# Moving the adaLN sums of one transformer block to other places among the gate logits and the levels of a triangular solve

## The chip, the cores and the metric

The kernel runs on one core of one Trainium2 chip, as one launch. The metric is device time in microseconds (us). A profile of one execution goes with it: which instruction ran on which engine and when, and what each wait ended with. The engines are TensorE (PE in the rows; PEld is its weight load), VectorE (DVE), ScalarE (ACT), GpSimd (POOL) and SyncE (SP), which issues the transfers from HBM. Each engine takes its own instructions in a fixed order, so a waiting instruction holds up all that stand behind it.

## The reference

256 tokens of width 1024 pass two layers. What matters here is the first layer's modulation (adaLN) and its gated delta rule.

```python
mod = jax.nn.silu(c) @ w_ada[l] + b_ada[l]            # c: 1 x 1024, w_ada: 1024 x 6144
shift1, scale1, gate1, shift2, scale2, gate2 = jnp.split(mod, 6, axis=-1)
h = modulate(rmsnorm(x, norm1_w[l]), shift1, scale1)
proj = h @ w_in[l]                                    # ..., d_q, d_k, d_v, d_z, d_a, d_b
qkv = silu(causal_dwconv(concat([d_q, d_k, d_v]), conv_w[l]))
beta = jax.nn.sigmoid(d_b)
g = -jnp.exp(a_log[l]) * jax.nn.softplus(d_a + dt_bias[l])
...
# gated_delta_rule, in chunks
decay = jnp.exp(jnp.where(tri_incl, g[..., :, None] - g[..., None, :], -jnp.inf))
a_mat = jnp.where(tri_strict, (k_beta @ swapaxes(k)) * decay, 0.0)
t_mat = lax.linalg.triangular_solve(eye + a_mat, eye, lower=True, unit_diagonal=True)
u = t_mat @ v_beta
...
x = x + gate1 * mix
ffn = hierarchical_moe(modulate(rmsnorm(x, norm2_w[l]), shift2, scale2), ...)
x = x + gate2 * ffn
```

After it come retention, the output projection, the router, 32 experts, a pooling mixer and a convolutional feed-forward layer.

## The kernel before

**The adaLN sums.** The 6144 columns of `w_ada` are twelve pieces of 512 columns (2 MB each), numbered 0 to 11. Pieces 0 to 3 (shift1, scale1) are needed for the first projection and are summed before it. Pieces 4 and 5 (gate1), 6 and 7 (shift2), 8 and 9 (scale2) and 10 and 11 (gate2) are needed much later: gate1 after the output projection, the others at the router or in the experts. A piece j has two steps. `s j` (`ada_sum`) is eight matmuls on TensorE (line 382), with the weight piece as the moving operand, and one VectorE instruction that takes the result out of PSUM: for the row pieces 4, 5, 10, 11 an addition onto `acc` (line 385), for the others a transpose (line 387). `e j` (`ada_end`) finishes it: for a row piece one matmul against ones (line 417) and a copy to `g1b` or `g2b`, by VectorE or ScalarE in turn (line 208 or 210); for a column piece four small matmuls (line 408) and an addition into `modT` (line 411).

**Where they stand.** The table `ADA` names places in the program and the steps put there; `ada("L1")` performs those of the place L1. The Tile scheduler then fixes each engine's order, so a step may slide past neighbours, and other work fills in around it.

```python
ADA = {'L1': 's4 s5', 'L2': 'e4', 'L3': 's6', 'L4': 'e5', 'L5': 's7 e6', 'E': 'e7', 'F': 's10', ...}
```

**The stage around it.** After the first projection (k, lines 509 and 568) come the gate logits: `psab` (line 605), its copy `abT` (line 208), two matmuls (line 611 before, 612 after), and a chain of small VectorE instructions with two exponentials on ScalarE (lines 613 to 638) that ends in `gg`. From `gg` come the decays `Dm` (lines 651 to 661) and the matrix `Am` (line 689). The solve inverts 32x32 blocks in five levels, 0 to 4: each is 32 tiny matmuls `Zc,Am` (line 705 before, 706 after), a masked product `Q` on VectorE (line 716), 32 tiny matmuls `Q,Xc` (none at level 0), a subtraction into `Zc` (line 723) and a transpose (line 725), after which stands the place `L0` to `L4`. Joining the blocks follows (lines 735 to 771, place `L5` in the middle), then the products with v (lines 783 to 808; the place `E` is ahead of line 788).

**What fills in.** The projections of v and then of q run beside it as `products`: triples of matmuls of 256 columns (line 290). Each piece of weights (128x512) is first split into a high part `wh` on ScalarE (line 281) and a low part `wl` on GpSimd (line 284). There are four buffers of each (NFS=4), so the sixth split waits until the products of the second are done. The convolution of v (line 568, three taps for each of four parts, on VectorE; lines 562, 563, 571 on ScalarE) runs there as well.

**Loads.** Weights lie in rings of 2 MB slots. SyncE issues the loads in one fixed order (`LOADS`), each when its slot is free: piece 8 goes into the slot of piece 4, w1 of `w_in` into that of piece 6, and so on, and the expert weights stand behind them.

Of the kernel before, what the change touches and what calls it, by code (L numbers as in the profile page):

```python
# [32 lines left out]
L4 = 5  # L33
# [12 lines left out]
SLOTS_MOE = 'ehg'  # L46
ADA_ACT = ()
SIDE = {3: 8, 7: 9}
ADA = {'L1': 's4 s5', 'L2': 'e4', 'L3': 's6', 'L4': 'e5', 'L5': 's7 e6', 'E': 'e7', 'F': 's10', 'G': 'e10', 'J': 's11', 'K': 'e11'}
KPOOL = ()  # L50
VPRE = 2
NLATE = 3
# [127 lines left out]
def build(ctx, tc, io, out, dbg=None):  # L180
    nc = tc.nc
    V, S, G, PE = nc.vector, nc.scalar, nc.gpsimd, nc.tensor
# [8 lines left out]
    def bank(tag=None):  # L191
        return pp.tile([128, 512], F32, name="ps", tag=tag or ptag[0])
# [12 lines left out]
    def copy(dst, src):  # L205
        _alt[0] ^= 1
        if _alt[0]:
            V.tensor_copy(dst, src)
        else:
            S.activation(dst, src, AF.Copy)  # L210
# [182 lines left out]
    def ada_sum(j, rows=False):  # L393
        for _ in ada_steps(j, rows, False):
            pass
# [58 lines left out]
    def ada(at):  # L454

        for step in ADA.get(at, "").split():
            j = int(step[1:])
            if step[0] == "s":
                ada_sum(j, j in (4, 5, 10, 11))
            else:  # L460
                ada_end(j)

    def ada_end(j):
        if j in (4, 5, 10, 11):
            ada_rows(j, (g1b if j < 6 else g2b)[:, 512 * (j % 2 if j > 9 else j - 4):][:, :512])
        else:
            ada_cols(j)
# [138 lines left out]
                      start=kk == 0, stop=kk == 1)  # L606
    abT = dp.tile([128, T], F32, name="abT")
    copy(abT, psab[:, :T])
    psab2 = bank()
    for t in range(2):  # L610
        PE.matmul(psab2[:, 8 * t:8 * t + 8], lhsT=abT[:, 128 * t:128 * t + 128], rhs=cfv("sel32"), start=True, stop=True)
# [727 lines left out]
    def tt(shape, name, bufs=None, tag=None, dtype=F32):  # L1339
        return tl.tile(shape, dtype, name=name, tag=tag or name, **({"bufs": bufs} if bufs else {}))  # L1340
# [7 lines left out]
    s4 = tt([128, 2, 2], "s4")  # L1348
    s5 = tt([128, 2, 2], "s5")
# [184 lines left out]
```

## Time and profile before

| what | us |
|---|---|
| median of three runs | 896.58 |
| lowest and highest | 892.93, 896.63 |
| the profiled execution | 897.43 |
| its span, first to last instruction | 895.6 |
| experts begin (first matmul of line 1285) | about 253 |
| gate logits and solve (lines 611 to 788) | about 53 to 106 |

TensorE is busy for 848.5 us of the span (95%), VectorE 398.5, ScalarE 272.5, GpSimd 146.6. In a row of the timeline the first number is the start in us, the second how long it (or the merged run of xN) took; brackets tell the idle time of the engine before it and what ended it. fp32 matmuls appear as two records each, so eight matmuls of line 382 are x16.

### The profile page before, as it was taken

How to read it: one execution, taken by the hardware profiler on the slowest of the kernel's cores; microseconds unless marked ns; L12 is line 12 of the kernel's file. 1: busy time of each engine (PE TensorE's matmuls, PEld its weight loads, DVE VectorE, ACT ScalarE, POOL GpSimd, SP SyncE). 2: the span in 40 equal slices, each digit the busy share in tenths (PEclk: the TensorE clock that was granted, in tenths of full speed). 3: DMA queues.
4: the chain of work that ended last, by engine and by line, in shares of the span. 5: the costliest groups of instructions: out<-in, count | busy, mean ns of one | idle time of the engine just before them, and what ended most of it. 6: DMA issues, size and time to landing. Idle time of an engine off the chain costs nothing.

```text
span 895.6 us, 12945 instructions
## 1 busy us (share of the span) xinstructions
PE 848.5 (95%) x5337; PEld 537.7 (60%) x5337; DVE 398.5 (44%) x750; ACT 272.5 (30%) x512; POOL 146.6 (16%) x109
## 2 busy tenths in 40 slices
PE   3998999989989999999999998989998999999998
PEld 0685788767734334343443444334334999999996
DVE  2577587586512122221222221122214877666664
ACT  2243154364401101010110101001015565555552
POOL 0234331162000000000000000000000033523525
PEclk9988899999999999999999999999999999999999
DMA  9982769767589999999999999999999744453001
GB/s 374 420 359 97 283 255 380 289 256 324 189 314 412 420 429 430 427 426 429 426 428 430 425 430 425 429 426 429 415 410 428 331 187 190 165 211 142 1 2 47
DMA packets 26111, 288.54 MB, mean 322 GB/s; under 512 B 3008, under 2 KB 3264, under 8 KB 9792
## 3 DMA queue, kind: packets, MB, share of 16 engines
q1 hardware_dynamic: 26048, 287.66, 78.1%
q8 instruction: 44, 0.72, 0.3%
q14 instruction: 19, 0.16, 0.1%
HBM read 286.60 MB, written 1.05 MB: 321 GB/s over the span
## 4 chain that ended last, share of the span: by engine, by line
PE 56%; DMA 14%; DVE 1%; ACT 0%; issue 0%; SPq 0%
PE ps L290 21%; PE ps L1285 18%; DMA wt<-in_w 14%; PE ps L1313 9%; PE ps L1244 3%; PE ps L1221 2%; PE ps L1396 1%; PE ps L1301 1%; PE ps L1415 1%; PE ps L1051 1%; PE ps L1386 0%; PE ps L1233 0%; DVE x L1517 0%; PE ps L1231 0%; ACT gh L1433 0%
## 5 line engine op out<-in xcount | busy, mean ns | idle before, releaser
L1285 PE MATMUL ps<-wt,x 128*64 128x512 f32 x1024 | 228.8, 598 | 8.0 <-DMA wt<-in_w 6.9
L1285 PEld LDWEIGHTS ps<-wt,x 128*64 128x64 f32 x1024 | 72.8, 138 | 155.6 <-issue 138.4
L281 ACT ACTIVATE wh<-wt 128x512 fp32r<-128x512 f32 (+1 forms) x138 | 113.4, 831 | 91.9 <-PE ps L290 83.8
L1313 PE MATMUL ps<-wt,hidT 128*64 128x512 f32 x512 | 113.8, 595 | 2.9 <-issue 1.9
L284 POOL TENSOR_TENSOR wl<-wt,wh 128x512 fp32r<-128x512 f32 (+1 forms) x52 | 94.7, 1834 | 90.8 <-ACT wh L281 88.3
L290 PE MATMUL ps<-gh,wh 128*128 128x256 f32 x352 | 98.5, 280 | 0.7 <-ACT gh L1433 0.7
L284 DVE TENSOR_TENSOR wl<-wt,wh 128x1024 fp32r<-128x1024 f32 (+1 forms) x86 | 83.8, 986 | 33.8 <-ACT wh L281 33.6
L290 PE MATMUL ps<-gl,wh 128*128 128x256 f32 x352 | 98.2, 279 | 0.0
L290 PE MATMUL ps<-gh,wl 128*128 128x256 f32 x352 | 98.2, 279 | 0.0
L1294 DVE SCALAR_TENSOR_TENSOR hid<-ps,gs,hid 128x512 f32<-128x512 f32 x16 | 12.0, 752 | 192.1 <-PE ps L1285 192.1
L1313 PEld LDWEIGHTS ps<-wt,hidT 128*64 128x64 f32 x512 | 40.9, 137 | 62.7 <-issue 58.9
L290 PEld LDWEIGHTS ps<-gh,wh 128*128 128x128 f32 x352 | 66.0, 188 | 1.1 <-ACT gh L1433 0.9
L290 PEld LDWEIGHTS ps<-gh,wl 128*128 128x128 f32 x352 | 66.1, 188 | 0.0
L290 PEld LDWEIGHTS ps<-gl,wh 128*128 128x128 f32 x352 | 65.9, 187 | 0.2
L1048 POOL TENSOR_TENSOR dg<-ca,sm 128x512 f32<-128x512 f32 x4 | 4.1, 1040 | 336.3 <-PE ps L1285 308.7
L1324 ACT ACTIVATE Yh<-ps 128x512 fp32r<-128x512 f32 x30 | 17.9, 597 | 107.7 <-DVE ps L1322 63.3
L1322 DVE TENSOR_TENSOR ps<-ps,g2b 128x512 f32<-128x512 f32 x30 | 21.0, 700 | 60.1 <-PE ps L1313 60.1
L1487 DVE SCALAR_TENSOR_TENSOR yf<-ps,sm,yf 128x254 f32<-128x254 f32 x88 | 42.0, 479 | 11.1 <-ACT yf L1484 9.9
L1492 POOL TENSOR_TENSOR yf<-yf 128x256 f32<-128x256 f32 x22 | 19.5, 887 | 140.4 <-ACT yf L1491 140.4
L1290 ACT ACTIVATE hid<-ps 128x512 f32<-128x512 f32 x16 | 9.6, 597 | 108.0 <-PE ps L1285 108.0
L217 ACT ACTIVATE x<-ps,modT,A 128x256 f32<-128x256 f32 x32 | 17.8, 563 | 68.6 <-PE ps L1221 68.6
L382 PE MATMUL ps<-wt,srep 128*32 128x512 f32 x160 | 26.2, 798 | 12.2 <-DMA wt<-in_w_ada 12.2
(383 smaller groups left out, 1280.8 us busy)
## 6 DMA issues: line engine op xcount, KB each, us to landing
wt<-in_w SPq DMA_DIRECT2D x86, 2048.0 KB, 22.2
wt<-in_w_ada SPq DMA_DIRECT2D x12, 2048.0 KB, 13.8
wt<-in_ffn_w_in SPq DMA_DIRECT2D x11, 2048.0 KB, 7.9
wt<-in_w SPq DMA_DIRECT2D x40, 512.0 KB, 10.2
wt<-in_w_in SPq DMA_DIRECT2D x7, 2048.0 KB, 14.4
wt<-in_ffn_w_out SPq DMA_DIRECT2D x5, 2048.0 KB, 8.4
wt<-in_w_out SPq DMA_DIRECT2D x2, 2048.0 KB, 8.0
wt<-in_w_in SPq DMA_DIRECT2D x2, 1024.0 KB, 20.1
```

The costliest lines, as they stand in the source:

```text
L281: S.activation(hi, src, AF.Copy)
L284: (eng or V).tensor_tensor(lo, src, hi.bitcast(F32), op=ALU.subtract)
L290: PE.matmul(ps, lhsT=a, rhs=b, start=first and n == 0, stop=last and n == 2)
L382: PE.matmul(ps[32 * q:32 * q + 32, :], lhsT=srep[:, 2 * q + kk, :], rhs=w[:, 2 * q + kk, :], start=kk == 0, stop=kk == 1)
L1221: PE.matmul(ps[d - d % 2][:, d % 2, :], lhsT=x[:, t, 128 * d:128 * d + 128], rhs=OH[:, t].rearrange("p g s -> p (g s)"), start=t == d % 2 ...
L1244: PE.matmul(res[t, c], lhsT=oT[:, 128 * t:128 * t + 128], rhs=y, start=False, stop=False)
L1285: PE.matmul(ps[64 * g:64 * g + 64, :], lhsT=xg[:, k, 128 * (p % 2) + 64 * g:128 * (p % 2) + 64 * g + 64], rhs=wt[p, nm, g][:, k, :], start ...
L1313: PE.matmul(py[c][64 * g:64 * g + 64, :], lhsT=hidT[:, f, 64 * g:64 * g + 64], rhs=wt[p, "w2", g][:, f, 512 * c:512 * c + 512], start=f == ...
L1322: V.tensor_tensor(py[c], py[c], g2c, op=ALU.mult)
L1324: S.activation(yh, py[c], AF.Copy)
L1487: V.scalar_tensor_tensor(y[:, sh:], ps[:, :T - sh], cw[:, 3 * m + tap:3 * m + tap + 1], y[:, sh:], op0=ALU.mult, op1=ALU.add)
L1492: G.tensor_tensor(ys[0], ys[0], ys[1], op=ALU.mult)
```

## The change

The table gets other places for the steps of pieces 4 to 7, and a new place `P` is put between the copy of `abT` and the two matmuls that take it. The steps s10, e10, s11, e11 stay.

```diff
-ADA = {'L1': 's4 s5', 'L2': 'e4', 'L3': 's6', 'L4': 'e5', 'L5': 's7 e6', 'E': 'e7', 'F': 's10', 'G': 'e10', 'J': 's11', 'K': 'e11'}
+ADA = {'P': 's4', 'A': 'e4', 'L0': 's5', 'L1': 's6 e5', 'L2': 's7 e6', 'L3': 'e7', 'F': 's10', 'G': 'e10', 'J': 's11', 'K': 'e11'}
...
     copy(abT, psab[:, :T])
+    ada("P")
     psab2 = bank()
```

The place `A` stands after `Dm` and ahead of the sum of squares of k (line 588). The new line moves every later line number up by one.

The first place that matters is ScalarE around the gate logits. Here `y` is the convolved k (its silu), `wh` a split of v's weights, and ACT_TABLE_LOAD the load of the table for the exponentials `beta` and `na` of the gate logits. Before:

```order
L571 ACTIVATE y<-y 128x256
L281 ACTIVATE wh<-wt 128x512
L571 ACTIVATE y<-y 128x256
L281 ACTIVATE wh<-wt 128x512
L571 ACTIVATE y<-y 128x256 x2
L615 ACT_TABLE_LOAD
L615 ACTIVATE beta<-ab 128x8
L622 ACTIVATE na<-na 128x8
```

After:

```order
L571 ACTIVATE y<-y 128x256
L281 ACTIVATE wh<-wt 128x512
L571 ACTIVATE y<-y 128x256 x3
L281 ACTIVATE wh<-wt 128x512
L616 ACT_TABLE_LOAD
L616 ACTIVATE beta<-ab 128x8
L623 ACTIVATE na<-na 128x8
```

The sixth split of v's weights (the second `wh` shown) has moved from ahead of the last two silus to behind them, right ahead of the table load. On TensorE the eight matmuls of s4 now stand ahead of line 612, and 17 products of v are ahead of line 612 where 32 were ahead of line 611.

The second place is TensorE from the second half of level 1 to level 2. `Q,Xc` and `Zc,Am` are the tiny matmuls of the solve, `wt,srep` the sums, `acc,ca` the end of a piece. Before:

```order
L705 MATMUL ps<-Q,Xc 32x16 x32
L382 MATMUL ps<-wt,srep 32x512 x16
L705 MATMUL ps<-Zc,Am 32x16 x32
```

followed by five products, level 2's `Q,Xc` and one matmul of line 417. After:

```order
L706 MATMUL ps<-Q,Xc 32x16 x32
L382 MATMUL ps<-wt,srep 32x512 x8
L417 MATMUL ps<-acc,ca 128x512
L706 MATMUL ps<-Zc,Am 32x16 x32
```

Of the sixteen matmuls of s4 and s5 that stood here, none is left; the eight of s6 and the one of e5 stand here instead. The eight of s5 are between the two halves of level 0 and level 1's first matmuls, the eight of s7 with e6 are ahead of level 3, e7 ahead of level 4.

The third place is VectorE in level 1, from the transpose that ends level 0 to the one that ends level 1; `y<-raw` are taps of v's convolution. Before:

```order
L725 STREAM_TRANSPOSE Xc<-Zc 128x128 x2
L568 SCALAR_TENSOR_TENSOR y<-raw,sm,y 128x253
L716 TENSOR_TENSOR Q<-ps,cf 128x64 x2
L568 SCALAR_TENSOR_TENSOR y<-raw,sm,y 128x254
L568 SCALAR_TENSOR_TENSOR y<-raw,sm,y 128x253
L723 TENSOR_TENSOR Zc<-Zc,ps 128x32x2 x2
L725 STREAM_TRANSPOSE Xc<-Zc 128x128 x2
```

After:

```order
L726 STREAM_TRANSPOSE Xc<-Zc 128x128 x2
L568 SCALAR_TENSOR_TENSOR y<-raw,sm,y 128x253 x2
L568 SCALAR_TENSOR_TENSOR y<-raw,sm,y 128x254
L385 TENSOR_TENSOR acc<-acc,ps 128x512
L717 TENSOR_TENSOR Q<-ps,cf 128x64 x2
L568 SCALAR_TENSOR_TENSOR y<-raw,sm,y 128x255
L568 SCALAR_TENSOR_TENSOR y<-raw,sm,y 128x254
L724 TENSOR_TENSOR Zc<-Zc,ps 128x32x2 x2
L726 STREAM_TRANSPOSE Xc<-Zc 128x128 x2
```

Two more taps and the addition of s5 now stand ahead of level 1's `Q`. The order of the loads on SyncE is the same.

## Rows read from the trace of the kernel before

**Rows 1.** The page's chain of work that ended last, by engine.

```profile
PE 56%; DMA 14%; DVE 1%; ACT 0%; issue 0%; SPq 0%
```

**Rows 2.** Busy time by stretch: engines (instructions), granted clock, DMA share, GB/s.

```profile
235.00:253.00 18.00, 16.49 (x88) 9.35 (x87) 9.76 (x42) 8.58 (x17) 0.00 (x0) 1.00 0.54 192
300.00:460.00 160.00, 159.19 (x792) 68.75 (x792) 36.33 (x65) 20.39 (x37) 0.00 (x0) 1.00 1.01 427
```

**Rows 3.** What TensorE waited for, 46 to 112 us: total, times, longest.

```profile
PE ps L705 <- issue: 2.5, 1, 2.5
...
PE ps L705 <- DVE Zc L723: 0.8, 1, 0.8
```

**Rows 4.** Two stretches for line 290 alone (PE, PEld, clock), one for all engines.

```profile
48.00:51.00 3.00, 3.00 (x27) 3.00 (x27) 1.00 1.03 437
55.00:59.00 4.00, 4.00 (x21) 4.00 (x20) 0.50 0.84 356
...
91.00:94.00 3.00, 3.00 (x77) 1.23 (x69) 0.82 (x2) 0.00 (x0) 0.00 (x0) 0.50 0.02 5
```

**Rows 5.** Timeline of TensorE, merged: start, us, line, what.

```profile
32.46 3.64 PE L382 MATMUL ps<-wt,srep 128*32 128x512 f32 x32
...
53.40 1.02 PE L611 MATMUL ps<-cf,abT 128*128 128x8 f32 x4 [2.06 <-DVE abT L208]
62.09 0.28 PE L642 MATMUL ps<-gg,cf 128*128 128x8 f32 x2
62.91 1.88 PE L654 MATMUL ps<-gm,ca 128*128 128x512 f32 x4
65.10 1.90 PE L588 MATMUL ps<-ca,sq 128*128 128x64 f32 x16
...
75.60 6.12 PE L382 MATMUL ps<-wt,srep 128*32 128x512 f32 x32
...
83.75 1.12 PE L417 MATMUL ps<-acc,ca 128*128 128x512 f32 x2
...
87.69 0.71 PE L705 MATMUL ps<-Zc,Am 32*32 32x16 f32 x34 [2.45 <-issue]
...
89.36 3.64 PE L382 MATMUL ps<-wt,srep 128*32 128x512 f32 x16
...
105.19 1.05 PE L788 MATMUL ps<-vb,Z 128*128 128x128 f32 x8
```

**Rows 6.** Timeline of ScalarE around the gate logits.

```profile
50.36 0.64 ACT L281 ACTIVATE wh<-wt 128x512 fp32r<-128x512 f32 x1 [0.47 <-PE ps L290]
...
54.27 1.28 ACT L615 ACT_TABLE_LOAD   x1
55.56 0.21 ACT L615 ACTIVATE beta<-ab 128x8 f32<-128x8 f32 x1
```

**Rows 7.** Timeline of VectorE, gate logits and level 1 of the solve.

```profile
55.80 0.17 DVE L616 TENSOR_SCALAR beta<-beta 128x8 f32<-128x8 f32 x1 [0.76 <-ACT beta L615]
...
61.07 0.17 DVE L638 SCALAR_TENSOR_TENSOR gg<-xa,ea 128x8 f32<-128x8 f32 x1
...
74.36 0.34 DVE L716 TENSOR_TENSOR Q<-ps,cf 128x64 f32<-128x64 f32 x2
74.62 2.63 DVE L568 SCALAR_TENSOR_TENSOR y<-raw,sm,y 128x254 f32<-128x254 f32 x2
...
77.86 1.62 DVE L568 SCALAR_TENSOR_TENSOR y<-raw,sm,y 128x255 f32<-128x255 f32 x4
79.40 0.67 DVE L385 TENSOR_TENSOR acc<-acc,ps 128x512 f32<-128x512 f32 x1
```

**Rows 8.** DMA queues from 85.2 to 87.8 us: packets, MB, share; q8 brings instructions.

```profile
q8 instruction: 1, 0.02, 2.2%
```

**Rows 9.** SyncE's issue of piece 4, and its time to landing (last number).

```profile
25.64 0.33 SPq L200 DMA_DIRECT2D wt<-in_w_ada  x1
...
wt<-in_w_ada SPq DMA_DIRECT2D x1, 2048.0 KB, 20.6
```

## The prediction, made before the changed kernel was run

> **What bounds the kernel now.** I read the chain of work that ended last first [rows 1]: it lies on TensorE for 56% of the span and on transfers for 14%, and the transfers are expert weights. So the second question is whether the front, up to the experts, is paced by engines or by loads. The table by stretch answers it [rows 2]: in the last 18 us ahead of the experts the transfers run at 192 GB/s, and inside them at 427. The loads wait for slots there, and slots come free when TensorE has used them. A microsecond saved or lost in the front therefore moves the start of the experts, the release of their slots and the end by the same amount. That holds for the gate logits and the solve too, as long as TensorE has enough products behind them; it has, since after line 788 it runs products almost without a gap.
>
> In the stage itself TensorE loses time in two ways. One is waiting [rows 3, 5]: 2.06 us for `abT`, 2.45 us in the middle of level 3 ("issue"), 0.8 us in level 1. The other is the granted clock: it is 0.5, the lower level (1.2 GHz), in 55 to 59 and in 91 to 94 us [rows 4], and a third time under the x32 of line 382 at 75.60, which take 6.12 us where the same x32 took 3.64 at 32.46 [rows 5]. A product takes 3.00 / 27 = 0.11 us at the full clock and 4.00 / 21 = 0.19 us at the half one [rows 4]. Eight sums (x16) take 1.82 us at full clock (half of 3.64 for x32) and 3.64 us at half [rows 5]. Each of the three came behind idle time or behind tiny matmuls with gaps. The third of the 0.5 stretches has the x16 at 89.36 in it, at 3.64 us.
>
> **The change part by part.** I follow the moments at which the parts of the solve start. A plus is later than before.
>
> *A, gate logits: +2.4 us.* The place P looks as if it filled the 2.06 us hole ahead of line 611. It does not: s4 takes 1.82 us, but 15 products leave the place (15 x 0.11 = 1.7 us), so the hole stays about 2 us, and with it the fall of the clock behind it. Piece 4 is there in time (25.64 + 20.6 = 46.2 us [rows 9]; wanted at 49.4, which is the start of the old hole, 51.3, less s4 and a product). The products now behind line 612 hold the sixth split: it needs the buffer that the 24th product frees. Before, that was at 50.36 us [rows 6]. Now seven of these products come after line 612, which ends at 54.4: 7 x 0.19 plus pipeline gives about 56.1. The split takes 0.64, the table load behind it 1.28, and `beta` follows: 56.1 + 0.64 + 1.28 + 0.25 = 58.3 us, where VectorE went on at 55.80 [rows 6, 7], so +2.5. At full clock it would be +1.9. `gg` was ready at 61.24 and TensorE took it at 62.09 [rows 5, 7], so 0.85 is slack: +1.65 at line 643. Then e4 stands ahead of line 588: 1.12 us [rows 5], for three or four products that leave (about -0.4). The sum is +2.4. Bounds: +1.0 (full clock and e4 beside other work) to +3.2 (no slack).
>
> *B, level 0: 0.* s5 takes the place of six products, 1.82 - 0.7 = 1.1 us more, of which 0.8 us was waiting for `Zc` [rows 3], and the rest lies ahead of the first half only. Bounds 0 and +0.9.
>
> *C, level 1: +1.55.* Two more taps and the addition of s5 stand ahead of `Q`: 2 x 0.44 + 0.67 [rows 7]. The four taps at 77.86 took 1.62 together, the two at 74.62 took 2.63 while GpSimd was splitting. I take the short price for the extra ones, since GpSimd should be done with its run of splits by then; at the long one (1.3 each) C is +3.3. What is late next is TensorE, which waits for `Q` with five products only.
>
> *D, from level 1 to level 2: -1.6.* Before, 6.12 us of sums stood here at a mostly half clock. Now x16 and one line 417: 1.82 + 1.12 = 2.9 us at full, twice that, 5.9, at half. TensorE idles for over a microsecond in front of `Q,Xc`, so I take the middle, 4.5. Bounds -3.2 and -0.2. Level 2 starts at about 84.0 instead of 81.7.
>
> *E, level 2 and the start of level 3: -0.5.* The 2.45 us stall goes, and so does the matmul of e4 that stood in level 2 (-1.12). In come s7 (+1.82), two VectorE instructions of 128x512 ahead of `Q` (2 x 0.67, half of it hidden), one product more and part of a half-clock stretch (+0.6). Of the stall: a packet of the instruction queue lies inside it [rows 8], and no engine that TensorE waits for was late. Level 2's second half, line 417 and level 3's first half followed each other there without anything slow between; now three products or more, and s7, stand between these bursts. So I take the stall as gone. The bound is that it stays (E = +1.9). The Trainium skill, "Runtime: NRT & Kernel Launch", section "Instruction fetch mechanics", says that instructions come in blocks and that the cost of crossing into the next is mostly hidden; by that, the 2.45 us would not come from a fetch, and E would keep it. The packet in the gap speaks against it.
>
> *F, level 3 to level 4: -2.6.* Before, s6 stood here at half clock, 89.36 to 93.0 [rows 5], of which about 0.7 us would have gone by anyway, until level 3's subtractions and transposes were done (two pairs of small VectorE instructions like the pair at 74.36, 0.34 each [rows 7]): 2.9 us on the path. Now only e7's small matmuls are there; two VectorE instructions of s7's end cost +0.3.
>
> *G, level 4 and the joining of blocks: 0.* e5 (line 417) and s7 with e6 leave this part, 1.1 us on the path. The last half of v's convolution now lands here, with taps between `Q` and `Zc` that wait for ScalarE (+0.6), and eleven more products (half of 11 x 0.11 on the path, +0.5). Bounds -1.1 and +1.3.
>
> At line 789: +2.4 + 0 + 1.55 - 1.6 - 0.5 - 2.6 + 0 = -0.75, so 104.4 instead of 105.19. *H:* six more products are done by then than before, 6 x 0.11 = -0.7 for the product-bound stretch behind. The sum is -1.45 us. Pieces 8, 10 and w1, w0 can load earlier, since s4 to s7 free their slots earlier; piece 7 loads some 2.5 us later with the last split. Neither was waited for, so both are worth nothing. GpSimd's two `acc` seeds for pieces 10 and 11 move up among its splits of q's weights, which TensorE needs only behind line 789.
>
> Against the profiled execution: 897.43 - 1.45 = 896.0. That execution is 0.85 above the median, so I go by the median: 896.58 - 1.45 = 895.1, rounded to 895.0.
>
> **The rivals.**
>
> *Faster: the clock holds.* If the sums between the bursts keep the clock up through levels 1 and 2, D goes to its bound (-1.6 more) and E loses its half-clock part and with full-clock bursts another 1.2 in all; A at its full-clock price gives 0.6: 3.4 us more, 891.6. For it: sums are dense work, and x16 now stands in each gap. Against it: the gap ahead of `Q,Xc` in level 1, and the hole ahead of line 612, which stays.
>
> *Slower: the clock falls behind the gate logits.* TensorE now runs out of products ahead of line 643: 49 of them from 54.3, 31 or so at 0.19 and the rest at 0.11, end at 62.2 to 62.8, and `gg` comes at 63.7. That is an idle time of 0.9 to 1.5 us that was not there. If it grows to the 2.06 us of the hole ahead of line 611, after which the clock was 0.5, then line 655 (1.88), e4 (1.12), line 588 (1.90) and the work of line 689, which is the same size, run at half: between 3.0 (the first two double) and 6.8 us (all). I take 5: 895.0 + 5 = 900.0, which is 3.4 slower than before. Against it: the hole as I work it out stays under 2.06.
>
> *The stall stays or moves* to levels 3 and 4, where now nothing slow stands between the tiny matmuls: +2.45, so 897.5, no difference. For it: from level 3 on the bursts are closer than before. Against it: products stand between nearly all of them.
>
> *The gain never arrives:* something behind line 788 that does not move, 896.6. The trace speaks against it: between line 788 and the experts none of TensorE's waits ends with a weight load. That the sums stay where they were is excluded by the order shown above.
>
> **How the numbers follow.** The forecast has 0.42, with its own range 892.5 to 898.0 from the bounds of A, D and E taken together (not all at one end). The faster case has 0.20, the slower one 0.15, the stall 0.18, the rest 0.05. The predicted time is the forecast's, 895.0. The range reaches to most of the faster and half of the slower cases: 890.5 to 900.0. Half a per cent, about what a measurement of this kernel can tell from no change, is 4.5 us: below 892.1 or above 901.1. Most of the faster case and a tenth of the forecast are below: 0.19. Above: a third of the slower case, some of the stall together with C's long price: 0.10. Within: 0.71.
>
> **What would show it.** A: `beta` at about 58 us and `gg` at 63.5, with the sixth split right ahead of the table load; wrong if `gg` is at 61. The granted clock near 53 to 60 still 0.5. C: level 1's `Q` about 4 us later than 74.4. D: 4 to 5 us from the end of `Q,Xc` to level 2. E: no idle "issue" of 2 us in level 3. F: level 4 starts within 1 us of level 3's transposes. Line 789 at 104 to 105. The forecast is wrong if line 789 is ahead of 102 or behind 107, and its last step is wrong if line 789 has moved by one amount and the first expert matmul, at 253 before, by another.

## The result, and the profile after

The changed kernel takes 907.0 us (median of 4 runs, 905.79 to 907.36) where the kernel before, run beside it, takes 895.62 (892.93 to 896.63): a ratio of 1.0133, 95% interval 1.0104 to 1.0162. It is slower by 1.3%, and outside the predicted range. The profiled execution took 907.36 us, its span 905.2 (897.43 and 895.6 before).

The front up to the experts shows where. This is the timeline of TensorE in the changed kernel (start, length, line, what; in brackets the idle time before it and what ended it); it answers to [rows 5], with line numbers behind the new line one higher:

```profile
51.58 0.53 PE L612 MATMUL ps<-cf,abT 128*128 128x8 f32 x4
...
61.69 0.56 PE L643 MATMUL ps<-gg,cf 128*128 128x8 f32 x2 [3.61 <-DVE gg L639]
...
63.54 3.62 PE L655 MATMUL ps<-gm,ca 128*128 128x512 f32 x4
66.94 1.57 PE L417 MATMUL ps<-acc,ca 128*128 128x512 f32 x2
68.35 1.90 PE L588 MATMUL ps<-ca,sq 128*128 128x64 f32 x16
...
72.95 0.44 PE L706 MATMUL ps<-Zc,Am 32*32 32x16 f32 x32
...
79.26 0.73 PE L706 MATMUL ps<-Q,Xc 32*32 32x16 f32 x64 [1.60 <-DVE Q L717]
...
82.82 0.73 PE L706 MATMUL ps<-Zc,Am 32*32 32x16 f32 x64
...
89.38 0.19 PE L408 MATMUL ps<-acc,ca 128*32 128x4 f32 x1 [1.83 <-issue]
89.50 0.73 PE L706 MATMUL ps<-Zc,Am 32*32 32x16 f32 x64
...
95.85 0.29 PE L706 MATMUL ps<-Q,Xc 32*32 32x16 f32 x4 [4.45 <-issue]
...
96.29 0.62 PE L706 MATMUL ps<-Zc,Am 32*32 32x16 f32 x32
...
101.49 0.41 PE L706 MATMUL ps<-Q,Xc 32*32 32x16 f32 x14 [2.15 <-issue]
...
102.55 0.64 PE L736 MATMUL ps<-Zc,Am 32*32 32x32 f32 x16
...
117.18 1.91 PE L789 MATMUL ps<-vb,Z 128*128 128x128 f32 x8
```

The hole ahead of line 612 is gone, and a wait of 3.61 us for `gg` is there instead. Just ahead of level 3, within level 3 and within level 4 are three idle times that end with "issue", that is, with nothing that the profile shows: 1.83 + 4.45 + 2.15 = 8.4 us, where the kernel before had one of 2.45 [rows 3]. Line 789 starts at 117.18 us instead of 105.19, 12.0 us later.

The second thing is the clock. Stretches of the changed kernel (all engines' busy time and instructions, then granted clock, DMA share, GB/s), which answer to [rows 2, 4]:

```profile
235.00:253.00 18.00, 17.70 (x96) 13.31 (x96) 9.57 (x36) 8.33 (x18) 0.00 (x0) 1.00 0.59 224
300.00:460.00 160.00, 159.19 (x799) 69.98 (x798) 36.79 (x65) 19.87 (x37) 0.00 (x0) 1.00 1.01 427
91.00:94.00 3.00, 0.40 (x47) 0.30 (x34) 0.53 (x2) 0.50 (x1) 0.00 (x0) 0.66 1.03 437
93.00:119.00 26.00, 21.01 (x283) 17.94 (x284) 9.96 (x27) 3.91 (x11) 5.15 (x7) 0.50 0.21 88
```

From 92 to 119 us the clock is at its lower level without a break: 27 us, where before each fall lasted some 7 us. It falls in the longest of the three idle times, and TensorE's work behind it runs at half speed all through level 4 and the joining of the blocks. In 91 to 94 us the transfers move 437 GB/s; before it was 5 [rows 4].

For the moments below, TensorE in the kernel before:

```profile
69.70 0.44 PE L705 MATMUL ps<-Zc,Am 32*32 32x16 f32 x32
...
81.65 0.73 PE L705 MATMUL ps<-Zc,Am 32*32 32x16 f32 x64
...
84.81 0.43 PE L705 MATMUL ps<-Zc,Am 32*32 32x16 f32 x30
...
92.94 1.05 PE L705 MATMUL ps<-Zc,Am 32*32 32x16 f32 x64
...
244.99 7.09 PE L1285 MATMUL ps<-wt,x 128*64 128x512 f32 x32
253.19 7.09 PE L1285 MATMUL ps<-wt,x 128*64 128x512 f32 x32 [1.12 <-ACTq L1173]
```

Moment by moment, against before: level 0 starts 3.25 us late (72.95 us; 69.70 before), level 2 1.2 (82.82), level 3 1.8 (89.50; taken against 87.69, where its matmuls went on behind the stall, as the first 30 records of it stand at 84.81 before), level 4 3.35 (96.29), line 736 6.2 (102.55; 96.34 before), line 789 12.0.

The experts' first matmuls come 11.7 us later: 256.66 us against 244.99. (About 253 us, given above as the experts' beginning, is where they go on after a wait of 1.12 us.) The end of the span is 9.6 us late. The experts' stretch is as dense as before. In the chain of work that ended last, transfers now have 6% instead of 14% [rows 1]. The 2 us between 11.7 and 9.6 do not lie in one place: the same matmuls of the experts are 13.4 us late at 274 us of the kernel before and 11.4 at their end. The chain of the changed kernel:

```profile
PE 63%; DMA 6%; DVE 1%; issue 0%; ACT 0%; SPq 0%
```

### The profile page after: what moved, and what is told of

Its sections match the earlier page's. It is cut to its first block, busy times and chain, and to the rows that moved or that the text cites. A ratio compares the mean times of both kernels' runs of the same rounds, so it can differ in the third digit from the quotient of the medians.

```text
span 905.2 us, 12941 instructions
## 1 busy us (share of the span) xinstructions
PE 851.2 (94%) x5337; PEld 540.0 (60%) x5337; DVE 396.6 (44%) x750; ACT 272.3 (30%) x512; POOL 146.6 (16%) x109
## 4 chain that ended last, share of the span: by engine, by line
PE 63%; DMA 6%; DVE 1%; issue 0%; ACT 0%; SPq 0%
PE ps L1286 21%; PE ps L290 20%; PE ps L1314 11%; DMA wt<-in_w 6%; PE ps L1245 3%; PE ps L1222 3%; PE ps L1397 1%; PE ps L1302 1%; PE ps L1416 1%; PE ps L1052 1%; PE ps L1234 0%; PE ps L1387 0%; PE ps L1232 0%; DVE x L1518 0%; ACT gh L1434 0%
## 5 line engine op out<-in xcount | busy, mean ns | idle before, releaser
L290 PE MATMUL ps<-wh,hfh 128*128 128x512 f32 x88 | 34.8, 396 | 0.0
## 6 DMA issues: line engine op xcount, KB each, us to landing
wt<-in_w SPq DMA_DIRECT2D x40, 512.0 KB, 10.2
```

Of the source, the lines that this page charges most:

```text
L290: PE.matmul(ps, lhsT=a, rhs=b, start=first and n == 0, stop=last and n == 2)
```

## The experiments

**Two theories for the idle times.** TensorE's instructions come in packets of 16 KB through the DMA queue q8. Counted in the trace (matmuls, weight loads and semaphore instructions), the matmuls behind the stalls lie 256 instructions apart, at the same places of that count in every run: each stall is at a boundary between two such blocks. *Loads:* s6 and s7 come earlier and free their slots earlier, so w1, w0 and piece 10 flow under levels 2 to 4, and the packet that a crossing calls for waits behind them. *Density:* with no sums left between the tiny matmuls, a block is used up faster than the next can come, whatever else flows. SyncE's issues of the changed kernel (w1 and w0, then piece 10) show that the loads are there; before, w1 and w0 were issued at 93.07 us and piece 10 at 100.49:

```profile
81.90 0.80 SPq L200 DMA_DIRECT2D wt<-in_w_in  x2
87.58 39.05 SPq L200 DMA_DIRECT2D wt<-in_w_ada  x2
```

All runs but two, before_heavy and spread1, which are told in the text, with what their profiled executions show (line 789: the start of the first matmul with v, whatever its line number there; stalls: sum of "issue" on TensorE, 46 to 125 us; low clock: us at the lower level, 46 to 130 us; ratio: against the kernel before on the same chip):

| kernel | line 789 | stalls | low clock | median | ratio, 95% interval |
|---|---|---|---|---|---|
| before | 105.19 | 2.45 | 20.5 | 895.62 | |
| changed | 117.18 | 8.4 | 34.1 | 907.00 | 1.0133, 1.0104 to 1.0162 |
| gate_l4 | 111.19 | 3.2 | 23.9 | 902.58 | 1.0086, 1.0061 to 1.0111 |
| gate_all | 109.06 | 1.6 | 27.3 | 900.72 | 1.0087, 1.0042 to 1.0131 |
| dense | 114.89 | 6.7 | 20.6 | 904.63 | 1.0100, 1.0071 to 1.0128 |
| gate_dense | 105.74 | 0.9 | 10.2 | 898.81 | 1.0040, 1.0016 to 1.0064 |
| late67 | 109.07 | 0.5 | 24.0 | 901.43 | 1.0077, 1.0048 to 1.0106 |
| p_only | 110.38 | 5.5 | 20.5 | 896.96 | 1.0035, 1.0005 to 1.0065 |
| no_p | 117.51 | 7.6 | 30.7 | 907.82 | 1.0155, 1.0121 to 1.0188 |
| before_heavy2 | 115.83 | 8.8 | 30.7 | 922.16 | 1.0312, 1.0282 to 1.0342 |
| swap_before | 107.92 | 5.2 | 13.6 | 897.08 | 1.0012, 0.9984 to 1.0041 |
| p_gate | 106.19 | 0.9 | 20.5 | 901.95 | 1.0074, 1.0051 to 1.0097 |
| spread_gate | 100.28 | 0.7 | 10.2 | 909.05 | 1.0171, 1.0125 to 1.0217 |
| spread_l4 | 98.84 | 0.4 | 6.8 | 896.50 | 1.0022, 1.0000 to 1.0044 |
| spread_w1f | 101.78 | 1.0 | 6.8 | 891.95 | 0.9968, 0.9941 to 0.9996 |

**gate_l4: the loads held back, the places as changed.**

```diff
-LOADS = '... a7e a8f w1h w0e a10e a9f o0e Xf Xe'
+LOADS = '... a7e a8f'
+LOADS1 = 'w1h w0e a10e a9f o0e Xf Xe'
...
         ada("L%d" % lev)
+        if lev == 4:
+            nc.sync.dma_start(held, Xc[0:1, :, 0, 0:4])
+            loads(LOADS1)
```

> The changed kernel, with the weight loads that stand behind piece 8 (w1, w0, piece 10 and so on) held back by a tiny transfer out of Xc until level 4 of the solve has ended; the order on TensorE is that of the changed kernel. Theory 1 (loads): the instruction fetches start late because they share the transfers with 6 MB of weights, so TensorE runs dry at block boundaries in levels 3 and 4. It expects the three stalls of 1.83, 4.45 and 2.15 us (8.4 in sum) to shrink to under 3 us in sum, the clock to be up for most of 92 to 118 us, line 789 at 104 to 109 us instead of 117.2, and a time of 895 to 900 us. Theory 2 (density): blocks of tiny matmuls are used up faster than they can be fetched, whatever else is loading. It expects the three stalls to stay within 2 us of their sum and a time of 905 to 909 us.

Stalls of 1.52, 1.43 and 0.23 us, 3.2 in sum; 902.58 us, 4.4 less than the changed kernel, but above what theory 1 gave. One load of `w_in` (2 MB; the rows don't say whether w1 or w0) had been issued ahead of the gate (81.15 us), and the stall of 1.52 stands where it flows. The clock still stayed low, 91 to 112 us. So the loads have a part in the stalls, but are not all of the loss.

**gate_all: both w1 and w0 held.**

```diff
+                elif name in ("w1h", "w0e"):
+                    d[n] = rings[name[2]].tile([128, 8, 512], F32, name="wt", tag="wt")
+                    nc.sync.dma_start(d[n][0:1, 0, 0:8]..., Xc[0:1, :, 0, 0:4])
+                    nc.sync.dma_start(d[n], io[src][n])
```

> The changed kernel with both w1 and w0 (and all that stands behind them) held until level 4 of the solve has ended: in the run before this one w1 had slipped ahead of the gate, and a stall of 1.5 us stood where its packets were. TensorE's order is that of the changed kernel to beyond line 789. Loads theory: the stalls in levels 2 to 4 sum to less than 1.5 us. Of the clock two readings are open. If it fell because of the idle time in the stalls, it is now up for most of 90 to 112 us, the joining of the blocks (from line 736 to line 789) takes 8 to 10 us instead of 14.6, and the time is 893 to 898 us. If it fell because the sums, the densest work of this stretch, have left levels 3 and 4 and the joining, it is at its lower level for 15 us or more there, the joining stays at 13 to 15 us, and the time is 898 to 902 us.

The packet itself can be seen. In the changed kernel TensorE crosses into a block at 83.08 us; two stretches of its DMA queues, 83.1 to 87.1 and 87.1 to 88.2 us, of which only the second has an instruction packet:

```profile
DMA packets 83, 1.36 MB, mean 340 GB/s; under 512 B 0, under 2 KB 0, under 8 KB 0
...
DMA packets 30, 0.49 MB, mean 447 GB/s; under 512 B 0, under 2 KB 0, under 8 KB 0
q8 instruction: 1, 0.02, 5.3%
```

With the loads held the same crossing is at 82.24 us; 82.2 to 83.1 and 83.1 to 84.1 us:

```profile
DMA packets 0, 0.00 MB, mean 0 GB/s; under 512 B 0, under 2 KB 0, under 8 KB 0
...
DMA packets 1, 0.02 MB, mean 16 GB/s; under 512 B 0, under 2 KB 0, under 8 KB 0
q8 instruction: 1, 0.02, 7.7%
```

The packet starts 0.9 us behind the crossing instead of 4.1. Two stalls are left, then the start of the joining and line 797 (789 of the changed kernel):

```profile
89.91 0.24 PE L712 MATMUL ps<-Q,Xc 32*32 32x16 f32 x4 [1.37 <-issue]
...
93.37 0.41 PE L712 MATMUL ps<-Q,Xc 32*32 32x16 f32 x14 [0.24 <-issue]
...
94.43 0.64 PE L744 MATMUL ps<-Zc,Am 32*32 32x32 f32 x16
...
109.06 1.91 PE L797 MATMUL ps<-vb,Z 128*128 128x128 f32 x8
```

So a little of the density theory holds too: with nothing else flowing, a block of tiny matmuls can still run out, for 1.4 us here. Of the clock the second reading came out: low for 20 us from 90.6 us on, the joining 14.6 us long as in the changed kernel.

**dense and gate_dense: idle matmuls where s6 and s7 had stood,** in the changed kernel and in gate_all.

```diff
-... 'L3': 'e7',
+... 'L3': 'd e7', 'L5': 'd',
...
+            if step == "d":
+                ps = bank("pa")
+                for kk in range(8):
+                    PE.matmul(ps[32 * (kk // 2):32 * (kk // 2) + 32, :], lhsT=srep[:, kk, :],
+                              rhs=ca[:, 0:512], start=kk % 2 == 0, stop=kk % 2 == 1)
+                continue
```

> The changed kernel with eight idle matmuls of the sums' size (32 x 512, over the constants) behind level 3 and eight behind the first half of the joining, where s6 and s7 stood in the kernel before; loads as early as in the changed kernel. They are 3.6 us of work at full clock, 7.3 at half. Dense-work theory: the clock is up again before line 736 or soon behind it, the joining takes 9 to 11 us with its eight matmuls instead of 14.6 without, and the time is 900 to 905 us, below the changed kernel in spite of the added work. Idle theory: the stalls under the loads keep the clock down (two stalls of 2 us or more remain), the joining takes 16 us or more, and the time is 908 to 914 us.

904.63 us: work was added, and line 789 (795 here) came 2.3 us earlier, at 114.89 us. The time did not rise; that it fell by itself is not shown, as the intervals of the two ratios overlap. The stalls stayed (1.48, 4.18, 1.08 us), as the loads were not touched; the low clock in this stretch fell from 27.3 to 13.7 us. The joining shrank by 1.5 us, to 13.1, since it met one of the low stretches (102.5 to 109.3 us); the theory gave 3.6 to 5.6.

> Both at once: w1 and w0 held until level 4 has ended, and the sixteen idle matmuls of the sums' size behind level 3 and in the joining. With the loads held alone the stalls fell to 1.6 us in sum but the clock stayed at its lower level for 20.4 us from 90.6 us on; with the idle matmuls alone it was at the lower level for 13.7 us in that stretch, against 27.3 in the changed kernel. If both causes are real and separate, stalls stay under 2 us and the lower clock in 88 to 112 us is 10 us or less; line 789 comes at 105 to 109 us in spite of 3.6 to 5.5 us of added work, and the time is 896 to 901 us. If the matmuls only cost what they take, line 789 is at 111 to 114 us and the time 903 to 906 us.

898.81 us, and line 789 (803 here) at 105.74 us, 11.4 earlier than in the changed kernel and 0.55 later than before, with sixteen matmuls more. The granted clock of 90 to 115 us (the third number from the end) in gate_all, dense and gate_dense:

```profile
90.00:115.00 25.00, 24.76 (x317) 21.67 (x318) 11.42 (x30) 5.17 (x13) 6.95 (x9) 0.59 0.62 254
...
90.00:115.00 25.00, 19.68 (x368) 11.37 (x359) 10.29 (x31) 3.93 (x11) 4.53 (x7) 0.73 0.35 147
...
90.00:115.00 25.00, 24.60 (x360) 16.91 (x352) 13.01 (x30) 5.06 (x13) 7.80 (x9) 0.86 0.62 254
```

The four kernels make a square: line 789 at 117.18 (neither), 109.06 (loads held), 114.89 (dense matmuls), 105.74 (both):

```profile
114.89 1.16 PE L795 MATMUL ps<-vb,Z 128*128 128x128 f32 x8
...
105.74 1.16 PE L803 MATMUL ps<-vb,Z 128*128 128x128 f32 x8
```

Up to there holding the loads is worth 8 to 9 us, dense matmuls 2 to 3 net of their own time, and together 11.4, about their sum. So both causes show, and the loads are the larger. The ratios stand in the same order (1.0133, 1.0087, 1.0100, 1.0040), but only both together are clear of the changed kernel's interval, and even then a loss of 0.4% in time is left.

**before_heavy2: the loads added to the kernel before.**

```diff
+        if lev == 1:
+            V.tensor_copy(seen, Xc[0:1, :, 0, 0:4])
+            nc.sync.dma_start(held, seen)
+            for n in range(3):
+                nc.sync.dma_start(spill[n], io["w_ada"][8])
+            loads(LOADS1)
```

> The kernel before with the 6 MB of idle transfers behind piece 8, this time gated through a copy of its own, so that the levels do not wait for the gate (in the earlier form the transfer read Xc itself, and the order on TensorE changed from level 3 on). TensorE's order is that of the kernel before through level 3 and nearly so behind it. Loads theory: instruction fetches behind the blocks crossed between 82 and 100 us start 3 us or more late, the stalls sum to 5 us or more instead of 2.45, and the time is 899 to 906 us. Density theory: one stall of 2 to 3 us as before, 894 to 898 us.

Three stalls where the kernel before has one, then line 798:

```profile
88.62 0.62 PE L709 MATMUL ps<-Zc,Am 32*32 32x16 f32 x32 [3.49 <-issue]
97.50 0.87 PE L709 MATMUL ps<-Zc,Am 32*32 32x16 f32 x49 [3.50 <-issue]
104.52 0.84 PE L745 MATMUL ps<-Zc,Am 32*32 32x32 f32 x22 [1.76 <-issue]
115.83 1.05 PE L798 MATMUL ps<-vb,Z 128*128 128x128 f32 x8
```

The loads alone make them, with the sums where they were. The time, 922.16 us, is far above what was expected: besides the 10.6 us up to line 789, the experts' first matmuls come 152 us behind it instead of 140. There TensorE waits for splits of weights, once for 5.7 us; that the real weights were late behind 6 MB of idle ones is likely, but is not shown by itself. The earlier form, before_heavy, was expected at 900 to 908 us if loads are the cause, with 4 us or more of stalls, and at 895 to 898 if not. Its gate held up the levels themselves and changed TensorE's order; it took 915.72 us (ratio 1.0248, 1.0197 to 1.0299), with stalls of 8.3 us, and settles nothing by itself.

**late67 and p_only: parts of the change alone.**

```diff
 late67:
+ADA = {'P': 's4', 'A': 'e4', 'L0': 's5', 'L2': 'e5', 'L3': 's6', 'L5': 's7 e6', 'E': 'e7', ...}
 p_only:
+ADA = {'P': 's4', 'A': 'e4', 'L1': 's5', 'L3': 's6', 'L4': 'e5', 'L5': 's7 e6', 'E': 'e7', ...}
```

> The changed kernel's places for pieces 4 and 5 (s4 at P, e4 at A, s5 at L0, e5 at L2), while pieces 6 and 7 stay where the kernel before has them (s6 at L3, s7 and e6 at L5, e7 at E), so that w1 and w0 load late again. Theory 1 (loads): one stall of 2 to 4 us at most near levels 2 to 4, and a cost of 3 us from the gate logits (half clock behind the wait for gg): 897 to 901 us. Theory 2 (density): s6 between levels 3 and 4 spreads the tiny matmuls, so it expects few stalls too; the same 897 to 901 us. If the move of 6 and 7 were not the cause at all, 905 to 909 us.

With s6 and s7 back, w1 and w0 are issued at 92.50 us, there is one stall of 0.51, and level 4 starts at 92.37 us, 3.9 earlier than in the changed kernel. The time, 901.43, is at the upper end: level 0 is 4 us late, and the clock is low for 17 us between 82 and 103 us, although the sums are there. Sums at these places do not keep the clock up by themselves.

> The kernel before, with s4 at P and e4 at A alone; s5 at L1 and all behind it as before. It measures the part of the change at the gate logits. If that part costs what level 0 showed in the changed kernel (+3.25 us at level 0, from a wait of 3.61 us for gg and a clock at its lower level in 61 to 68 us), less the eight matmuls that leave level 1 (1.8 to 3.6 us), the time is 895 to 898 us; theory 1 expects no more than one or two stalls, as the loads of w1 and w0 wait for s6. A rival says that the gate logits alone make the loss: 903 us or more.

896.96 us, within what was expected. s5 and then s6 come a little earlier than before, w1 and w0 are issued at 88.94 us instead of 93.07, and one stall of 4.36 us stands behind that, in the joining.

**no_p: the change without its part at the gate logits.**

```diff
+ADA = {'L0': 's4 s5', 'L1': 's6 e4 e5', 'L2': 's7 e6', 'L3': 'e7', ...}
```

> The changed kernel without its part at the gate logits: s4 goes to L0, next to s5, and e4 to L1; the rest as changed. It prices that part. If the wait of 3.6 us for gg and the lower clock behind it come from s4 and the fifteen products that it pushes behind line 612, level 0 starts at 69.5 to 70.5 us instead of 72.95; with 1.8 to 3.6 us of s4 added to level 0 or 1, level 2 starts within 1 us of the changed kernel's 82.8, and the time is 903 to 907 us, as the stalls in levels 3 and 4 stay. If the gate logits were the cause of the whole loss: 896 to 899 us.

Level 0 starts at 70.23 us, as expected, but level 2 at 85.1, 2.3 later than in the changed kernel: the sums moved to levels 0 and 1 cost there what they had cost at P. 907.82 us: within the intervals, the changed kernel's time, so here the part at the gate logits is worth nothing that can be measured.

**swap_before and p_gate: other times for the loads.**

```diff
 swap_before (kernel before):
-LOADS = '... a6h a7e a8f w1h w0e a10e ...'
+LOADS = '... a6h a7e w1h w0e a8f a10e ...'
 p_gate (p_only, the gate of gate_all reading X64, also for piece 10):
+                    nc.sync.dma_start(d[n][0:1, 0, 0:8]..., X64[0:1, :, 0, 0:4])
```

> The kernel before with one change in the order of the loads: piece 8 stands behind w1 and w0 instead of ahead of them, so that it no longer flows under level 2 (it was landing at 82 to 87 us, when TensorE crossed into the block whose instructions came late). The order on TensorE is untouched. Loads theory: the stall of 2.45 us at 87.7 us goes (0.5 us or less is left), line 788 starts 1.5 to 2.5 us earlier, and the time is 891.5 to 893.5 us. Density theory: the stall stays within 0.7 us, and the time does not move.

My expectation missed: of w1 and w0 one was issued at 80.99 us, behind s5, and the other at 88.21, behind s6, as the slots came free, and piece 8 behind both at 88.63. So a load flowed under level 2 again. The stall at 85 us shrank to 0.43, and two others came where these loads flow, 1.43 at 89.81 and 3.35 at 96.28 us. The stalls followed the loads; line 788 came 2.7 us later, and the time did not move.

> The kernel with s4 at P and e4 at A alone (896.96 us), with w1, w0 and piece 10 held until the second join of the blocks has begun (a tiny transfer that waits for X64). There it had a stall of 4.36 us in the first join, with w1 and w0 loading from 88.94 us on, and two of 0.83 and 0.34. Loads theory: the 4.36 goes to about 0.5, and the time to 892 to 894 us, if w1 is still in time for the first split of q's weights at 114 us. Density theory: no change, 896 to 898 us.

The stall of 4.36 went, and line 789 came 4.2 us earlier (106.19). But the time rose by 5 us: behind it TensorE waits for splits of weights that come late (2.0 us at 121.83 us), and the experts start at 252.4 instead of 248.2. Holding the loads has a price.

**The sums one by one in the gaps of the solve.**

```diff
+ADA = {'L0': 's4', 'L1': 's5', 'L2': 'e4', 'L3': 's6', 'L4': 'e5', 'L5': 's7 e6', 'E': 'e7', ...}
```

> A candidate: the sums one by one in the gaps of the solve, none at the gate logits (s4 behind level 0, s5 behind level 1, e4 behind level 2, s6 behind level 3, e5 behind level 4, s7 and e6 in the joining, e7 at E), with w1, w0 and pieces 8 and 10 held until the second join has begun. Loads and dense-work theories together: no stall over 1 us, level 0 at 69.5 to 70.5 us, the lower clock no longer than the 20.5 us of the kernel before, and a time of 890 to 894 us. If the places of the sums cost more than the stalls: 896 to 902 us.

Line 789 at 100.28 us, 4.9 earlier than before and the earliest so far, and 909.05 us: a later weight of `w_in`, issued at 148.46 us instead of 140.17, is waited for by ScalarE, and TensorE waits for that. ScalarE and TensorE:

```profile
160.69 2.19 ACT L282 ACTIVATE wh<-wt 128x512 fp32r<-128x512 f32 x4 [14.42 <-DMA wt<-in_w_in]
...
161.37 0.80 PE L291 MATMUL ps<-wh,hh 128*128 128x512 f32 x1 [10.32 <-ACT wh L282]
```

> The sums one by one in the gaps of the solve, as in the run before with these places, which reached the first products with v at 100.28 us (105.19 in the kernel before) and then lost 14 us because w1, held until the second join, came too late for the splits of q's weights. Here w1, w0, piece 10 and piece 8 are held only until level 4 has ended, about 89 us. Loads theory: no stall over 1.5 us up to line 789, which comes at 100 to 103 us, no long wait for the splits behind it, and a time of 889 to 893 us. Rival: the loads released at 89 us meet the block crossed at 91.6 us and the joining has a stall of 3 to 4 us again; 893 to 897 us.

(The weight that came too late was this later one, not w1, as I had written.) Line 789 is the earliest of all, 98.84 us, but a wait of 2.7 us for a split is left behind it, and the median of ten runs, 896.50, is no gain.

> The same places; w1 takes the slot of piece 4, which s4 frees behind level 0, so it loads at about 72 to 80 us, ungated; piece 8 takes the slot that w1 had, and w0, piece 8 and piece 10 are held until the second join. Loads theory: one late fetch at the block crossed near 73 us (a stall of 0 to 3 us, as eight sums stand there), none behind it, no wait for w1; line 789 at 100 to 104 us, 889 to 894 us. Rival: w0 or piece 10, held late, are now what the q projections wait for: 896 us or more.

891.95 us, a ratio of 0.9968 (0.9941 to 0.9996): faster than both kernels, than the one before by 0.3%, which its interval only just clears. The same places with the loads of the kernel before, nothing held (spread1), were expected at 892 to 898 us by the loads and at 888 to 891 by the density theory. They gave 893.18 us and 0.9958 (0.9930 to 0.9986): the loads theory's range, but no slower than with loads held, so here holding loads earned nothing that can be measured. Its profiled execution was the longest of its ten, and no row of it is used.

## Why the prediction was wrong

*What bounds the front* was right in kind: the loss at line 789 reached the experts almost whole (12.0 to 11.7 us). The end got 9.6 of it. The 18 us that were read as lying ahead of the experts [rows 2] have 8 us of them in it; the ten from 235 to 245 us say the same, with 213 GB/s.

*A, +2.4 at level 0:* 3.25 measured, by another way. The hole did not stay and the split did not hold the chain: `beta` came at 55.21 us, not 58.3, and `gg` at 61.38. TensorE reached line 612 1.8 us earlier, ran out of products ahead of line 643 for 3.61 us, and the clock fell there: line 655 took 3.62 us instead of 1.88. At line 643 it was still 0.4 us ahead of before, where +1.65 was predicted; what was lost was lost behind it, by the lower clock and e4 (line 417, 1.57 us). That is the mechanism of the slower rival, without most of its price, since line 588 ran at full clock again (1.90 us). VectorE of the changed kernel, `beta` and `gg`:

```profile
55.21 0.17 DVE L617 TENSOR_SCALAR beta<-beta 128x8 f32<-128x8 f32 x1 [1.60 <-ACT beta L616]
...
61.38 0.17 DVE L639 SCALAR_TENSOR_TENSOR gg<-xa,ea 128x8 f32<-128x8 f32 x1
```

The hole itself can come and go without the change; the later start of level 0 does not (last section).

*B, C, D, together -0.05 up to level 2:* -2.1 measured. `Q` of level 1 came 4.6 us later than before (about 4 predicted), and the sums behind it ran at the full clock, so D was at its bound of -3.2.

*E and F, -3.1 up to level 4:* +2.2 measured, and here the argument broke. E came to +0.6, as a stall of 1.83 stands where one of 2.45 was to go, and F to +1.5. F without its stall is -2.9 (6.79 us from level 3 to level 4, less 4.45, against 5.25), close to the -2.6 predicted. The stalls undid it. Two sentences failed: "I take the stall as gone", and that the earlier loads of pieces 8, 10 and w1, w0 are "worth nothing", since nobody waited for them. Nobody did, but TensorE's own instructions share the transfers with them. I had seen the packet of instructions inside the stall [rows 8], and not asked what flowed beside it. The Trainium skill, "Runtime: NRT & Kernel Launch", section "Instruction fetch mechanics", calls the cost of crossing a block mostly hidden; the runs differ, with stalls of up to 4.45 us in the changed kernel. The rival of the stall had the places right, at +2.45, but by closer bursts and not by loads; the stalls summed to 8.4.

*G, level 4 and the joining, 0:* +8.6 measured, the largest miss, and a term that I priced at full clock without asking. 2.15 of it is the third stall; the rest goes with a clock at its lower level all the way. The sums that I counted only as time to be saved were the densest work there. gate_all and gate_dense tell the two apart: with 1.6 us of stalls left in all, the joining still took 14.6 us at the lower clock, and with dense matmuls as well all but 0.55 us of the loss at line 789 was gone. Why late67, with real sums at the same places, still had 17 us of low clock is open.

*The rivals* had no case in which the two meet; the slower one stopped at 900.0.

## What to carry to other kernels

When an edit frees a buffer earlier, look at what loads into it, and what TensorE does meanwhile: here a stretch of tiny matmuls used up its instructions faster than they arrived beside a full stream of weights. Before moving dense work out of such a stretch, price what is left at the lower clock, not at the one that the dense work had kept up. And a load that is held can have a price further on: p_gate and spread_gate lost there what they had won.

## What the runs showed of the hardware

*Instruction packets wait behind weights.* Over the kernel before, the changed one and fourteen others, 94 crossings of a block between 69 and 107 us, counted in the traces, fall into two groups by what flowed until the packet began. In 61 with under 40 GB/s it began 0.5 to 2.3 us after the crossing, 1.1 in the middle of them; in 33 with over 310 GB/s 2.5 to 6.9 us after it, 3.8 in the middle, but for two at 0.3 and 0.6. A stalled TensorE went on about 1.3 us after the packet had ended.

*Two engines slow each other, and a hole comes and goes with which one is slow.* In two kernels whose program is the same up to there, spread_l4 and spread_w1f, VectorE's eleven taps ahead of `abT` and GpSimd's two splits beside them took different times. VectorE, GpSimd and TensorE of spread_l4, then of spread_w1f:

```profile
45.37 7.17 DVE L574 SCALAR_TENSOR_TENSOR y<-raw,sm,y 128x253 f32<-128x253 f32 x11 [1.60 <-ACT raw L569]
49.16 2.71 POOL L285 TENSOR_TENSOR wl<-wt,wh 128x512 fp32r<-128x512 f32 x2 [3.02 <-ACT wh L282]
52.93 0.61 PE L618 MATMUL ps<-cf,abT 128*128 128x8 f32 x4 [2.06 <-DVE abT L209]
...
46.05 5.12 DVE L574 SCALAR_TENSOR_TENSOR y<-raw,sm,y 128x253 f32<-128x253 f32 x11 [1.59 <-ACT raw L569]
49.83 3.92 POOL L285 TENSOR_TENSOR wl<-wt,wh 128x512 fp32r<-128x512 f32 x2 [3.02 <-ACT wh L282]
61.13 0.56 PE L649 MATMUL ps<-gg,cf 128*128 128x8 f32 x2 [3.72 <-DVE gg L645]
```

Where VectorE is slow (7.17 us) the hole of 2.06 us stands ahead of line 618; where GpSimd is slow (3.92), the hole is gone and the wait for `gg` is 3.72. The kernel before was of the first kind in its profiled execution, the changed one of the second, so a part of A could be this and not the change.

The other runs speak against it: in all eight kernels with s4 at the place P, level 0 starts 26.4 to 27.4 us after the first of the eleven taps, whichever engine was slow, and each has a wait of 3.61 us for `gg`. In eight without it, spread1 left aside, it starts 23.2 to 23.9 us after that tap in the five with the hole of 2.06, and 23.5 to 25.5 in the three without (23.9 in the kernel before, 26.9 in the changed one).

The Trainium skill, "SBUF — State Buffer", section "Who interferes with whom", says that a VectorE instruction with two inputs in SBUF and a GpSimd instruction that reads SBUF contend for one pair of ports, and that the order of issue decides who blocks. The two traces agree that one of the two is slow where they run together: two of the taps take 1.53 and 1.48 us instead of 0.48, or the first split takes 2.48 us instead of 1.30. Which was issued first they do not tell, as in both the split's record begins 0.06 to 0.07 us ahead of a tap's.
